# Attention in steps of two key blocks, the query projection held back by one chunk, and another tile order in the last chunk

## The chip, the core and the metric

The kernel runs on one core of one Trainium2 chip. The metric is the device time of one execution in microseconds (us). Engines are named as in the profile: PE multiplies matrices, PEld loads its weights, DVE, ACT and POOL work elementwise, SP issues the DMAs.

## What is computed

Two layers work on 1040 tokens (16 learned ones ahead of 1024) of 1024 features. Each layer has a normalisation, one input projection, two groups of attention heads, gates and an output projection. Cut to what matters here:

```python
hn = rmsnorm(h, norm_gain[l])
dq, dk, dv, dg, fq, fk, fv, ff, fg = split(hn @ w_in[l])
# differential heads (4): two softmaxes, one subtracted from the other
p = softmax(dq @ dk.T * scale, masked by chunks of 64)
a = p[:, :, 0] - lam * p[:, :, 1]
do = rmsnorm(a @ dv, subln_gain[l]) * (1 - lam_init) * silu(dg)
# forgetting heads (8): one softmax with a bias per key, causal by token
s = fq @ fk.T * scale + cum_logf(query) - cum_logf(key)
fo = softmax(s, causal) @ fv * silu(fg)
h = h + concat(do, fo) @ w_out[l]
```

Matrix products are made from split operands: a value is written as hi + lo, and hi*hi, lo*hi and hi*lo are added up.

## The kernel before

The tokens are cut into nine tiles (`BS`, the first of 80 tokens, the next seven of 128, the last of 64) and these into three chunks c of three tiles. The heads come in eight pairs p: 0 to 3 are the differential heads (the "diff" stage), 4 to 7 hold two forgetting heads each (the "fox" stage), which the code tells apart by s. A **unit** (l, p, c, s) is the attention of one chunk of queries against its 3, 6 or 9 blocks of keys.

For a unit, `scores` makes the products of queries and keys of one query tile into PSUM buffers named sc (three of them), in up to three pieces. DVE adds the bias and keeps a running minimum (L629), ACT takes the exponential and its sum (L633), DVE the reciprocal (L636). In the fox stage POOL scales the row (L665). In the diff stage there are two such rows for a tile; POOL scales the one (L679) and DVE joins them (L681). The result stands in e. Then, for each block j of keys, `transp` turns the three tiles' parts of e on PE into one of two PSUM buffers tp; ACT copies them out as ath (L710) and DVE makes the rest atl (L711). `av` multiplies these by the values into po.

In the diff stage the fill's k and q are rotated on DVE (L400 to L403) with a table that a DMA loads into cb. What stands around all this on PE is the **fill**: products of the projections (pj) that the next pairs and the gates need. `fills` makes them in the order of `ORDER`, k, q, gate and v of each pair, and then the output projection, in portions of two of eight k-steps (six products). `layer` walks through `attention`, which yields a time that its next step needs and a key; by a clock of its own (`pe.t`) `layer` puts in fill until that time has come, or while a credit lasts. A fill generator that may not go on yields True, and then nothing is put in. It may not go on, among others, where q of pair p and chunk c would overwrite the buffer `qls[c]`, of which there is one for each chunk; the line is

```python
while c and p and (p - 1, c - 1) not in box["sc_ok"]:
```

where `sc_ok` holds the chunks whose scores are all in. The order of PE is the one in which these calls are made; the other engines' order comes from the framework's scheduler, and each engine works through its own in order.

In `attention` one unit's blocks run as t0 t1 a0 t2 a1 t3 and so on (t a transposition, a the products with v), and after every second step one score step of the next unit is put in, as far as buffers of e are there (`free`). A unit starts when its last scores are through (`u.ready`).

Of the kernel before, what the change touches and what calls it, by code (L numbers as in the profile page):

```python
# [49 lines left out]

LS0, LS1, LT, L1S, LROT, LFOX = 2.04, 0.0045, 2.41, 4.87, 6.0, 5.61
OT1, OT2, OT3, OW, OL = 2.46, 4.57, 2.54, 7.53, 4.52
CMAX, SLACK, RMIN, RMAX, STEP, FR0, FR1 = 3.17, 0.8, 0.03, 2.52, 2, 2, 2
COST = {"k": 10.4, "q": 10.4, "g": 10.4, "v": 24.0, "h": 0.0}
FADD = [0.0, -2.7, 0.0, 2.0, 0.0, 0.2, -0.7, 47.4]
ATT = [21.5, 21.5, 21.2, 21.5, 28.5, 28.5, 28.1, 28.9]
# [24 lines left out]
def trunk_kernel(ctx, tc, x, meta, norm_gain, w_in, fbias, lq1, lk1, lq2, lk2,  # L81
# [356 lines left out]
    def q_unit(l, p, acts, box):  # L438


        diff = p < 4
        q0 = (DQ if diff else FQ) + (p % 4) * P
        ws = load_w_all(w_in[l], [(q0, q0 + P)])
        for c in range(3):
            w = CE[c] - CS[c]
            while c and p and (p - 1, c - 1) not in box["sc_ok"]:
                yield True
            mb, o = [], skip(l, c)
            yield from mtile(ws, acts, c, mb, o)
            src, scale = (rotate(mb[0], c, -SCALE, o), 1.0) if diff else (mb[0], -SCALE)  # L450
            qq = [st("qq", CW, F32R, QB) for _ in range(2)]
            ql = qls[c]
            if o:
                for t in qq + ql:
                    nc.gpsimd.memset(t[:, :o].bitcast(F32), 0.0)
            for s in range(2):
                r, ro = halves(s)
                split(qq[s][r, o:w], ql[s][r, o:w], src[r, o:w], scale)
                nc.gpsimd.tensor_scalar(qq[s][ro, o:w], qq[s][r, o:w].bitcast(F32), 1.0, 1.0,  # L459
                                        ALU.mult, ALU.mult)  # L460
            box["q", p, c] = (qq, ql)
            when["q", p, c] = pe.t + (LROT if diff else LFOX)
            yield
# [175 lines left out]
    class Unit:  # L639


        def __init__(self, l, p, s, c, box):
            self.l, self.p, self.s, self.c, self.box = l, p, s, c, box
            self.w = CE[c] - CS[c]
            self.at = []
            self.tiles = range(3 * c, 3 * c + 3)
            self.nblk = 3 * c + 3
            self.diff = p < 4
            self.ev = {}
            self.ready = 0.0  # L650
            self.begun = False
# [4 lines left out]
        def score(self, j, m):  # L656
# [5 lines left out]
            if not self.diff:  # L662
                cb = self.box["cb", self.s]
                e, r, rows = scores(kt, q, self.s, j, ext, lambda a, b: cb[:, a:b], True)
                nc.gpsimd.tensor_scalar(e[rows, :ext], e[rows, :ext], r[rows, 0:1], 1.0,  # L665
                                        ALU.mult, ALU.mult)
                self.at.append((e, rows))
                self.ready = pe.t + LS0 + LS1 * ext
                return
            dm = self.box["dm"]  # L670
# [4 lines left out]
            if m == 0:  # L675
# [4 lines left out]
                                    neglam[rows, l:l + 1], ALU.mult, ALU.mult)  # L680
            nc.vector.scalar_tensor_tensor(e0[rows, :ext], e0[rows, :ext], r0[rows, 0:1],  # L681
                                           e[rows, :ext], ALU.mult, ALU.add)
            self.at.append((e0, rows))
            self.ready = pe.t + LS0 + 1.3 * LS1 * ext

        def geom(self, j):
# [9 lines left out]
        def transp(self, j):  # L696
            c, w = self.c, self.w
            kz, i0, n0, n1 = self.geom(j)
            tp = att_ps()
            for i in reversed(range(i0, 3 * c + 3)):  # L700
                e, rows = self.at[i - 3 * c]
                o = BS[i] - CS[c] - self.pad(i)
                tr(tp[:kz, o:BE[i] - CS[c]], e[rows, BS[j] - self.pad(j):BE[j]],
                   ident[rows, rows])
# [67 lines left out]
    def attention(l, box):  # L772
# [5 lines left out]
        def score(u, step):  # L778
            if not u.begun:
                u.begun = True  # L780
                if u.c == 0 and u.s == 0:
                    box["sp"] = u.p
                    for s in range(0 if u.diff else 2):
                        cb = box["cb", s] = big("cb", 2)
                        h = 2 * (u.p - 4) + s
                        dma(out=cb, in_=cscr[l, h:h + 1, :].to_broadcast([P, T]))
            u.score(*step)
# [8 lines left out]
        for i, u in enumerate(units):  # L796
# [5 lines left out]
            if nx and nx.p != u.p and not nx.diff:  # L802
                free = 0
            n = u.nblk
            seq = [("t", j) for j in range(TB)]
            for j in range(n):
                seq.append(("a", j))
                if j + TB < n:
                    seq.append(("t", j + TB))
            nt = 0  # L810
            yield u.ready, ("v", u.p, 0)
            box["vp"] = u.p
            for k, (what, j) in enumerate(seq):
                if late and pe.t >= late[0][0]:
                    late.pop(0)[1]()
                    yield 0.0, None
                if what == "t":
                    u.transp(j)
                    nt += 1
                else:  # L820
                    yield u.ev[j][2], ("v", u.p, j)
                    u.av(j)
                yield 0.0, None
                if todo and (nt == n or (free > 0 and nt >= FR0 and k % FR1 == FR1 - 1)):
                    free -= 1
                    yield 0.0, ("k", nx.p, nx.c)
                    yield 0.0, ("q", nx.p, nx.c)
                    score(nx, todo.pop(0))
                    yield 0.0, None
            for t0, f in late:  # L830
                yield t0, None
                f()
# [319 lines left out]
```

## Time and profile before

| | |
|---|---|
| median of 3 runs | 1616.0 us (1613.42 to 1619.95) |
| the profiled execution | 1615.97 us, its span 1614.2 us |
| granted TensorE clock, mean | 0.961 |
| PE busy | 1490.0 us, 92% |
| DVE, ACT, POOL busy | 1044.3, 825.2, 772.6 us |

Layer 0 has its diff stage at about 94 to 415 us, its fox stage at 415 to 694 us, layer 1 its own at 876 to 1203 and 1203 to 1484 us; between and behind them lies the output projection. A row of a timeline has start, duration, engine, line, operation, output and inputs with their forms, the count of merged instructions, and in brackets the idle time of the engine before it with what ended it. A PE duration holds the latency of the array too; the distance of two starts tells what one costs in a stream.

### The profile page before, as it was taken

To read this page: it belongs to the slowest core of one execution; us is meant where nothing else is said; L and a number is where in the kernel's file an instruction comes from. 1 tells how busy PE (TensorE), PEld (TensorE's weight loads), DVE (VectorE), ACT (ScalarE), POOL (GpSimd) and SP (SyncE) were. 2 spreads that over 40 slices of the span, in tenths; PEclk is the share of its full clock that TensorE was granted. 3 is DMA by queue.
4 is the path that set the end of the run, shared out by engine and by line. 5 is a ranking of instruction groups with operands and counts; after the bars stand their busy time and mean duration, and the time that the engine had idled before them with its cause. 6 is when DMAs were issued, how large, how long until landed. Compare 5 with 4: busy or idle time off the path is not lost.

```text
span 1614.2 us, 30133 instructions
## 1 busy us (share of the span) xinstructions
PE 1490.0 (92%) x9932; PEld 1425.6 (88%) x9932; DVE 1044.3 (65%) x3020; ACT 825.2 (51%) x2067; POOL 772.6 (48%) x1211
## 2 busy tenths in 40 slices
PE   5979999999999999798997989999999999988997
PEld 4878998899999999697987989898999999977897
DVE  6468677856665556667755765876667555656654
ACT  6445445544555556544333544554446555555553
POOL 3355355523543445375746443544345344545564
PEclk8999999999999999799998999999999999998899
DMA  8322122213220222554524221322122112253454
GB/s 248 76 74 71 50 71 62 73 26 47 62 61 23 66 65 79 156 173 133 165 66 93 55 77 26 90 54 62 31 67 50 46 43 75 58 151 92 119 168 135
DMA packets 170317, 134.80 MB, mean 84 GB/s; under 512 B 18456, under 2 KB 165456, under 8 KB 170160
## 3 DMA queue, kind: packets, MB, share of 16 engines
q1 hardware_dynamic: 170160, 132.87, 31.2%
q8 instruction: 79, 1.29, 0.3%
q14 instruction: 78, 0.64, 0.1%
HBM read 111.49 MB, written 21.33 MB: 82 GB/s over the span
## 4 chain that ended last, share of the span: by engine, by line
PE 68%; DVE 11%; DMA 7%; issue 5%; POOL 4%; ACT 3%; SPq 1%; DVEq 0%; POOLq 0%; ACTq 0%
PE pj L161 43%; PE sc L161 9%; PE po L161 8%; PE tp L165 7%; DMA cb<-in_rope_dram 3%; DMA tc<-nscr 2%; DVE e L629 2%; DVE kt L410 2%; DVE e L681 2%; DVE tc L383 1%; ACT e L633 1%; DMA e<-in_x_dram 1%; POOL wlo L245 1%; DMA wst<-in_w_in_dram 1%; PE sc L165 1%
## 5 line engine op out<-in xcount | busy, mean ns | idle before, releaser
L161 PE MATMUL pj<-acth,whi 128*128 128x320 f32 (+2 forms) x1536 | 515.7, 336 | 3.6 <-DVE hc L895 2.1
L161 PE MATMUL pj<-actl,whi 128*128 128x320 f32 (+2 forms) x1536 | 497.4, 324 | 0.1
L161 PE MATMUL pj<-acth,wlo 128*128 128x320 f32 (+2 forms) x1536 | 496.8, 323 | 0.0
L633 ACT ACTIVATE e<-e,mn 80x80 f32<-80x80 f32 (+8 forms) x288 | 225.4, 783 | 165.2 <-DVE mn L629 158.0
L161 PEld LDWEIGHTS pj<-acth,whi 128*128 128x128 f32 x1536 | 294.7, 192 | 6.1 <-POOL whi L243 2.6
L161 PEld LDWEIGHTS pj<-acth,wlo 128*128 128x128 f32 x1536 | 294.3, 192 | 0.6
L161 PEld LDWEIGHTS pj<-actl,whi 128*128 128x128 f32 x1536 | 293.2, 191 | 0.7 <-DVE actl L410 0.6
L245 POOL TENSOR_TENSOR wlo<-wst,whi 128x256 fp32r<-128x256 f32 (+1 forms) x320 | 248.4, 787 | 81.5 <-ACT whi L241 69.2
L710 ACT ACTIVATE ath<-tp 128x320 fp32r<-128x320 f32 (+8 forms) x432 | 167.1, 402 | 171.9 <-PE tp L165 165.7
L711 DVE TENSOR_TENSOR atl<-tp,ath 128x320 fp32r<-128x320 f32 (+8 forms) x432 | 190.4, 449 | 98.6 <-ACT ath L710 94.9
L165 PE MATMUL tp<-ident,e 128*128 128x128 f32 (+2 forms) x1080 | 184.0, 280 | 50.0 <-DVE e L681 27.9
L161 PE MATMUL sc<-kt,qq 128*128 128x296 f32 (+9 forms) x480 | 178.8, 375 | 18.7 <-POOL qq L459 13.7
L165 PEld LDWEIGHTS tp<-ident,e 128*128 128x128 f32 (+2 forms) x1080 | 137.7, 141 | 59.0 <-issue 24.3
L665 POOL TENSOR_SCALAR e<-e,rl 80x80 f32<-80x80 f32 (+2 forms) x144 | 110.9, 770 | 157.1 <-DVE rl L636 154.4
L241 ACT ACTIVATE whi<-wst 128x256 fp32r<-128x256 f32 (+1 forms) x304 | 123.6, 413 | 104.1 <-PE pj L161 66.2
L629 DVE CUSTOM_DVE_ANT_0 e<-sc,cb 128x336 f32<-128x336 f32 (+8 forms) x272 | 139.8, 515 | 52.7 <-PE sc L161 49.9
L161 PE MATMUL po<-ath,v 128*128 128x256 f32 (+5 forms) x576 | 168.8, 334 | 4.0 <-ACT ath L710 2.1
L161 PE MATMUL pj<-whi,acth 128*128 128x256 f32 (+3 forms) x576 | 166.2, 289 | 4.3 <-DVE v L410 3.7
L161 PE MATMUL pj<-wlo,acth 128*128 128x256 f32 (+3 forms) x576 | 163.3, 284 | 1.3 <-POOL wlo L245 0.7
L161 PE MATMUL pj<-whi,actl 128*128 128x256 f32 (+3 forms) x576 | 163.2, 283 | 1.3 <-POOL actl L386 1.1
L161 PE MATMUL sc<-kt,ql 128*128 128x296 f32 (+9 forms) x480 | 161.9, 339 | 0.0
L161 PE MATMUL po<-atl,v 128*128 128x256 f32 (+5 forms) x432 | 137.7, 319 | 8.0 <-DVE atl L711 5.8
(153 smaller groups left out, 2513.6 us busy)
## 6 DMA issues: line engine op xcount, KB each, us to landing
wst<-in_w_in_dram SPq DMA_DIRECT2D x256, 128.0 KB
wst<-in_w_out_dram SPq DMA_DIRECT2D x192, 128.0 KB
cb<-cscr SPq DMA_DIRECT2D x16, 520.0 KB
cb<-in_rope_dram SPq DMA_DIRECT2D x20, 320.0 KB
cb<-in_rope_dram SPq DMA_DIRECT2D x16, 384.0 KB
cb<-in_rope_dram SPq DMA_DIRECT2D x12, 336.0 KB
e<-in_x_dram SPq DMA_DIRECT2D x7, 512.0 KB
actl<-oscr SPq DMA_DIRECT2D x4, 768.0 KB
```

The lines of the kernel that those rows point to most:

```text
L161: nc.tensor.matmul(o, a, b, start=start, stop=stop)
L165: nc.tensor.transpose(o, a, idn)
L241: nc.scalar.activation(hi, sg_, AF.Copy)
L245: eng.tensor_tensor(lo, sg_, hi.bitcast(F32), ALU.subtract)
L383: nc.vector.scalar_tensor_tensor(t[:, :w], src, ng[:, l, k:k + 1], rb, ALU.mult, ALU.mult)
L410: nc.vector.tensor_tensor(lo, src, hi.bitcast(F32), ALU.subtract)
L629: nc.vector.tensor_tensor_reduce(e[rows, a:b], pt[rows, :b - a], bias(a, b)[rows, :], op0=ALU.add, op1=ALU.min, scale=1.0, scalar=3e38 if ...
L633: nc.scalar.activation(e[rows, :ext], e[rows, :ext], AF.Exp, scale=-1.0, bias=mn[rows, len(pcs) - 1:len(pcs)], accum_out=l[rows, 0:1])
L665: nc.gpsimd.tensor_scalar(e[rows, :ext], e[rows, :ext], r[rows, 0:1], 1.0, ALU.mult, ALU.mult)
L681: nc.vector.scalar_tensor_tensor(e0[rows, :ext], e0[rows, :ext], r0[rows, 0:1], e[rows, :ext], ALU.mult, ALU.add)
L710: nc.scalar.activation(ah[:kz, n0:w], tp[:kz, n0:w], AF.Copy)
L711: nc.vector.tensor_tensor(al[:kz, n0:w], tp[:kz, n0:w], ah[:kz, n0:w].bitcast(F32), ALU.subtract)
```

## The change

Three things. In `attention` a step is now two blocks wide: the products of two blocks one behind the other, then at once the transpositions of the next two, then one score step of the next unit (two in the diff stage). A late sum of a finished unit (`late`) comes behind the transpositions, no longer ahead of them. In `q_unit` the projection of q for chunk c waits until the scores of the pair before are in for this chunk, no longer for the one ahead of it. In the last chunk the query tiles are scored in the order 6, 8, 7, and every unit transposes its tiles in the order of their scores, where it was the reverse.

```diff
@@ q_unit
-            while c and p and (p - 1, c - 1) not in box["sc_ok"]:
+            while p and (p - 1, c) not in box["sc_ok"]:
                 yield True
@@ Unit.__init__
-            self.tiles = range(3 * c, 3 * c + 3)
+            self.tiles = (6, 8, 7) if c == 2 else range(3 * c, 3 * c + 3)
@@ Unit.transp
-            for i in reversed(range(i0, 3 * c + 3)):
-                e, rows = self.at[i - 3 * c]
+            for i in self.tiles:
+                if i < i0:
+                    continue
+                e, rows = self.at[i]
@@ attention
-            for k, (what, j) in enumerate(seq):
-                if late and pe.t >= late[0][0]:
-                    late.pop(0)[1]()
-                    yield 0.0, None
-                if what == "t":
-                    u.transp(j)
-                    nt += 1
-                else:
-                    yield u.ev[j][2], ("v", u.p, j)
-                    u.av(j)
-                yield 0.0, None
-                if todo and (nt == n or (free > 0 and nt >= FR0 and k % FR1 == FR1 - 1)):
+            for j0 in range(0, n + 1, TB):
+                done, group = range(max(j0 - TB, 0), j0), range(j0, min(j0 + TB, n))
+                for j in done:
+                    if j < n:
+                        yield u.ev[min(done[-1], n - 1)][2], ("v", u.p, j)
+                        u.av(j)
+                for j in group:
+                    u.transp(j)
+                yield 0.0, None
+                if late and pe.t >= late[0][0]:
+                    late.pop(0)[1]()
+                    yield 0.0, None
+                for _ in range(2 if nx and nx.diff else 1):
+                    if todo and (free > 0 or j0 + TB >= n):
...
+                        score(nx, todo.pop(0))
...
+            if n % TB:
+                yield u.ev[n - 1][2], ("v", u.p, n - 1)
+                u.av(n - 1)
```

Three places show what this makes of the engines' order. The first is PE in layer 0 ahead of unit (0, 6, 2, 0), the last chunk of pair 6; tp are the transpositions, pj is fill, po the products with v, sc the scores. Before, these rows stand at the start of the unit, and between its last score and here lie 30 products of fill:

```order
L161 MATMUL pj<-acth_249,whi 128x336
L161 MATMUL pj<-acth_249,wlo 128x336
L161 MATMUL pj<-actl_250,whi 128x336
L165 MATMUL tp<-ident,e 80x128 x3
L165 MATMUL tp<-ident,e 128x128 x3
L161 MATMUL sc<-kt,qq 128x424
L161 MATMUL sc<-kt,ql_85 128x424
```

After:

```order
L161 MATMUL sc<-kt,qq 128x488
L161 MATMUL sc<-kt,ql_84 128x488
L161 MATMUL sc<-kt,qq 128x488
L161 MATMUL sc<-kt,ql_84 128x488
L161 LDWEIGHTS cb_68
L161 MATMUL sc<-cb_68 128x128
L161 MATMUL po<-ath,v 128x256
L161 MATMUL po<-atl,v 128x256
L161 MATMUL po<-ath,v 128x256
L161 MATMUL po<-atl,v 128x256
L165 MATMUL tp<-ident,e 80x128 x3
L165 MATMUL tp<-ident,e 128x128 x3
```

The unit's last scores (tile 7) now stand four products of 256 columns ahead of its first transposition, and the fill is gone from there. The second place is PE in layer 0 at the start of pair 5, unit (0, 5, 0, 0). Before, the last scores of its tile 2 are followed by fill, 18 products of it up to the first transposition:

```order
L161 MATMUL sc<-kt,qq 128x336
L161 MATMUL sc<-kt,ql_80 128x336
L161 LDWEIGHTS cb_68
L161 MATMUL sc<-cb_68 128x128
L161 MATMUL pj<-acth_362,whi 128x384
L161 MATMUL pj<-acth_362,wlo 128x384
L161 MATMUL pj<-actl_363,whi 128x384
```

After:

```order
L161 MATMUL sc<-kt,qq 128x336
L161 MATMUL sc<-kt,ql_80 128x336
L161 LDWEIGHTS cb_68
L161 MATMUL sc<-cb_68 128x128
L165 MATMUL tp<-ident,e 80x80
L165 MATMUL tp<-ident,e 80x128 x2
L165 MATMUL tp<-ident,e 128x128 x2
```

Nothing stands between scores and transpositions any more. The third place is DVE in layer 0 behind the first two transpositions of unit (0, 1, 1, 0), a diff unit, where the scores of tile 6 follow on PE; atl is the rest of a transposed block, ms a sum per head, L629 takes a piece of the scores out of PSUM. Before:

```order
L711 TENSOR_TENSOR atl<-tp,ath 80x384
L629 ISA e,mn<-sc,cb 128x424
L629 ISA mn 128x1
L711 TENSOR_TENSOR atl<-tp,ath 128x384
L629 ISA e,mn<-sc,cb,mn 128x424
```

After (L711 is L714 there, L770 is L773):

```order
L714 TENSOR_TENSOR atl<-tp,ath 80x384
L773 COPY ms<-sc 80x1
L773 COPY ms<-sc 128x1
L714 TENSOR_TENSOR atl<-tp,ath 128x384
L773 COPY ms<-sc 128x1
L629 ISA e,mn<-sc,cb 128x424
L629 ISA mn 128x1
```

The first piece of the scores now stands behind both blocks' atl and the three copies.

## Rows read from the trace of the kernel before

**Rows 1.** The page: span, then busy time, share and count of PE.

```profile
span 1614.2 us, 30133 instructions
PE 1490.0 (92%) x9932; PEld 1425.6 (88%) x9932; DVE 1044.3 (65%) x3020; ACT 825.2 (51%) x2067; POOL 772.6 (48%) x1211
```

**Rows 2.** By stage: stretch, length, busy time (count) of PE, PEld, DVE, ACT, POOL; clock.

```profile
94.00:415.00 321.00, 302.84 (x2039) 294.16 (x2040) 231.66 (x684) 164.19 (x421) 146.02 (x205) 0.97 0.25 59
415.00:655.00 240.00, 237.79 (x1651) 227.04 (x1650) 141.31 (x449) 132.56 (x337) 109.70 (x196) 1.00 0.22 60
655.00:694.00 39.00, 27.68 (x158) 24.30 (x157) 26.74 (x79) 20.96 (x53) 17.44 (x33) 0.78 0.53 161
...
1203.00:1444.00 241.00, 237.69 (x1661) 227.05 (x1660) 142.43 (x451) 133.94 (x339) 111.90 (x208) 1.00 0.25 65
```

**Rows 3.** Who PE waited for: us in total, times, longest.

```profile
PE tp L165 <- DVE e L681: 27.9, 11, 3.9
PE tp L165 <- POOL e L665: 21.9, 5, 6.3
...
PE po L161 <- DVE atl L711: 5.8, 8, 2.9
```

**Rows 4.** Timeline of PE around unit (0, 6, 2, 0).

```profile
612.48 0.44 PE L161 MATMUL po<-atl,v 80*128 80x384 f32 x1 [0.33 <-DVE atl L711]
...
613.99 0.23 PE L161 MATMUL sc<-cb 128*128 128x128 bf16 x1
...
622.17 0.82 PE L165 MATMUL tp<-ident,e 128*80 128x128 f32 x6
```

**Rows 5.** Timeline of POOL there, the scaling of tile 7.

```profile
617.65 1.09 POOL L665 TENSOR_SCALAR e<-e,rl 128x976 f32<-128x976 f32 x1
```

**Rows 6.** Timeline ahead of unit (0, 5, 0, 0).

```profile
487.03 0.28 PE L161 MATMUL po<-ath,v 128*128 128x256 f32 x1
...
487.14 0.28 PE L161 MATMUL po<-atl,v 128*128 128x256 f32 x1
...
487.58 0.23 PE L161 MATMUL sc<-cb 128*128 128x128 bf16 x1
...
489.99 0.54 POOL L665 TENSOR_SCALAR e<-e,rl 128x336 f32<-128x336 f32 x1
```

**Rows 7.** Timeline of PE: the longest start of a unit of pair 7, layer 0.

```profile
677.70 1.08 PE L165 MATMUL tp<-ident,e 128*80 128x128 f32 x4 [5.58 <-POOL e L665]
```

**Rows 8.** Busy time in stretches of low granted clock, columns as in Rows 2.

```profile
309.40:316.20 6.80, 4.89 (x20) 4.86 (x21) 6.40 (x16) 2.63 (x6) 3.49 (x5) 0.50 0.25 63
244.50:247.90 3.40, 3.40 (x15) 3.38 (x15) 3.25 (x10) 2.08 (x6) 2.67 (x4) 0.50 0.25 89
```

**Rows 9.** Timeline: starts of diff units, and DVE ahead of the one at 311 us.

```profile
243.76 0.50 PE L165 MATMUL tp<-ident,e 128*80 128x128 f32 x3 [2.31 <-DVE e L681]
...
308.23 0.51 DVE L402 TENSOR_TENSOR tc<-tc,cb 128x336 f32<-128x336 f32 x1 [0.95 <-DMA cb<-in_rope_dram]
...
309.86 1.30 DVE L681 SCALAR_TENSOR_TENSOR e<-e,rl 128x1040 f32<-128x1040 f32 x1
...
311.31 1.47 PE L165 MATMUL tp<-ident,e 128*80 128x128 f32 x6 [3.88 <-DVE e L681]
```

**Rows 10.** Timeline of PE and DVE at the first blocks of unit (0, 0, 1, 0).

```profile
122.73 0.83 PE L165 MATMUL tp<-ident,e 128*80 128x128 f32 x6
122.91 0.28 DVE L770 COPY ms<-sc 80x1 f32<-80x1 f32 x3 [0.43 <-PE sc L161]
...
123.32 0.44 PE L161 MATMUL sc<-kt,qq 128*128 128x424 f32 x1
...
123.79 0.55 DVE L711 TENSOR_TENSOR atl<-tp,ath 80x384 fp32r<-80x384 f32 x1 [0.60 <-ACT ath L710]
123.79 0.36 PE L161 MATMUL sc<-kt,qq 128*128 128x424 f32 x1
...
124.26 0.58 DVE L629 CUSTOM_DVE_ANT_0 e<-sc,cb 128x424 f32<-128x424 f32 x1
```

More of the change, by code (lines that the diff above doesn't have):

```diff
@@ L52 @@
 OT1, OT2, OT3, OW, OL = 2.46, 4.57, 2.54, 7.53, 4.52
-CMAX, SLACK, RMIN, RMAX, STEP, FR0, FR1 = 3.17, 0.8, 0.03, 2.52, 2, 2, 2
+CMAX, SLACK, RMIN, RMAX, STEP = 3.17, 0.8, 0.03, 2.52, 2
 COST = {"k": 10.4, "q": 10.4, "g": 10.4, "v": 24.0, "h": 0.0}
@@ L644, in __init__ @@
             self.w = CE[c] - CS[c]
-            self.at = []
-            self.tiles = range(3 * c, 3 * c + 3)
+            self.at = {}
+            self.tiles = (6, 8, 7) if c == 2 else range(3 * c, 3 * c + 3)
             self.nblk = 3 * c + 3
@@ L666, in score @@
                                         ALU.mult, ALU.mult)
-                self.at.append((e, rows))
+                self.at[j] = e, rows
                 self.ready = pe.t + LS0 + LS1 * ext
@@ L682, in score @@
                                            e[rows, :ext], ALU.mult, ALU.add)
-            self.at.append((e0, rows))
+            self.at[j] = e0, rows
             self.ready = pe.t + LS0 + 1.3 * LS1 * ext
@@ L804, in attention @@
             n = u.nblk
[L805 to L810, printed above, removed]
             yield u.ready, ("v", u.p, 0)
             box["vp"] = u.p
-            for k, (what, j) in enumerate(seq):
+            for j0 in range(0, n + 1, TB):
[7 more added lines that the diff above has]
+                yield 0.0, None
                 if late and pe.t >= late[0][0]:
@@ L816, in attention @@
                     yield 0.0, None
-                if what == "t":
-                    u.transp(j)
-                    nt += 1
-                else:
-                    yield u.ev[j][2], ("v", u.p, j)
-                    u.av(j)
-                yield 0.0, None
-                if todo and (nt == n or (free > 0 and nt >= FR0 and k % FR1 == FR1 - 1)):
[L825 to L828, printed above, removed]
-                    yield 0.0, None
+                for _ in range(2 if nx and nx.diff else 1):
+                    if todo and (free > 0 or j0 + TB >= n):
+                        free -= 1
+                        yield 0.0, ("k", nx.p, nx.c)
+                        yield 0.0, ("q", nx.p, nx.c)
+                        score(nx, todo.pop(0))
[3 more added lines that the diff above has]
+                u.av(n - 1)
+                yield 0.0, None
             for t0, f in late:
```

## The prediction

> **What bounds the kernel now.** I read the page first, then busy time by stage, then who PE waited for, then the timeline at the starts of units. PE is busy for 92% of the span [rows 1], and the stages show where the other 8% lies. In both fox stages up to pair 7 PE is busy for 237.8 of 240 us and for 237.7 of 241, at clock 1.00 [rows 2]: nothing is left to be won there, and whatever is added to PE's waits comes out in full. In the diff stage it is 302.8 of 321 us, so 18 are idle, and in pair 7 of layer 0 27.7 of 39 at clock 0.78 [rows 2]. The waits have one main form: at the start of a unit the first transposition waits for its e, 27.9 us in 11 waits for DVE's L681 (diff) and 21.9 in 5 for POOL's L665 (fox) [rows 3]. Each of the long ones draws a stretch at half the clock behind it [rows 8]. So the question is whether the change shortens the starts of the diff units and pair 7, and what it does to the full fox stages.
>
> **The change part by part**, against the profiled execution's 1615.97 us, which is 0.03 off the median, so no correction is needed.
>
> *Products and transpositions in pairs.* The same instructions are issued. Six transpositions in a row take 0.59 us until the next product starts, 0.1 each [rows 10], and this run of six stands at the start of every unit of before already; pairing saves nothing and costs nothing in itself. (The Trainium skill, "TensorE: Matmul & The Clock Gate", Part 4, says that the full clock doesn't engage for transpositions; the fox stages at 1.00 speak against that here. Were it to decide, it is the fourth rival below.)
>
> *What the pair has to wait for.* Before, between block j's transposition and its product stood the product of the block ahead and the transposition of the block behind; now both blocks of a pair have only scores and fill between. In the planner each pair therefore asks for fill, and so fill is used earlier inside a unit and is short at the starts. Where no fill comes, the atl chain shows: the nearest row is 0.33 us [rows 4]. The order has 32 fox pairs with no fill between. Between nothing (the scores of the next unit cover it) and 0.5 us, I take 0.25: 8 us, from 0 to 16.
>
> *The starts of fox units.* This is the main term. By the order, the PE work between a unit's last score and its first transposition falls in six starts from 3 to 6 us to nearly nothing. Three are last chunks, (0,6,2,0), (1,4,2,0) and (1,6,2,0): q of pair 7 or 5 has come to its last chunk, which the new line lets on only when all scores of the pair are in, so no fill is there. Before, that start came without a wait: the score of tile 7 began its last product at 613.99, e was ready at 617.65 + 1.09 = 618.74 [rows 5], 4.75 us later, and PE had work until 622.17 [rows 4]. Now there is 0.04 for that product, four products of 256 columns at 0.11 each [rows 6], and two transpositions ahead of the one that waits, 0.22: 0.7 us of cover, so a wait of 4.0. Three times: 12 us. At (0,4,2,0) twelve products of fill stay, some 2.1 us of cover: 1.9. At the start of pairs 5 (both layers) and 7 (layer 0) the order has nothing between tile 2's scores and the transpositions: 487.58 to 489.99 + 0.54 = 490.53 is 2.95 us [rows 6], less 0.04 and 0.2 of transpositions: 2.7, three times 8.1. Together 22 us, from 17 (all chains a fifth shorter) to 26.
>
> *The clock behind them.* After a wait of 3.9 us PE ran 6.8 us at 0.50, busy for 4.89 of them, so about 2.4 were lost; after one of 2.3 us it ran 3.4 us at 0.50 and lost 1.7 [rows 8, 9]. Three starts at 2.4 and three at 1.7, the latter not always: 11 us, from 5 to 18.
>
> *Scores in pairs in the diff stage.* In unit c = 1 four pieces of scores now follow each other, and there are three sc buffers. In before the first piece's L629 started 0.94 us after the scores did, with one atl ahead of it [rows 10]; now a second atl (0.55) and three copies (0.28) stand ahead [rows 10]. So its end is at about 0.94 + 0.55 + 0.28 + 0.58 = 2.35 us. The fourth piece asks at 3 times 0.47 = 1.4, and some 0.3 later since the three late sums now stand ahead of the scores: a wait of 0.6 us, eight units, 5 us. Bounds: 0, if other work of PE comes between, and 10.
>
> *Starts of the diff units.* Starts of a first chunk lose or gain cover by the order, from 2.1 us less to 0.9 more, six of them: together 3 us more, from 0 to 6. Starts of a last chunk: the tile that comes last is now 976 keys wide in two pieces, no longer 1040 in three, and its scores stand two steps earlier, while DVE's order still has the rotation's L402, which waits for its table, ahead of the joining of e, as at 308.23 and 309.86 [rows 9]. By the order the starts of pair 1 have four fewer DVE instructions in between, the others as many as before. I take 4 us off, bounds 14 off and 5 on.
>
> *Pair 7.* Its long waits, 5.6 us as the longest of layer 0 [rows 7], stay, since the fill is still used up. The output projection's loads and splits move two to four blocks ahead, so the first start gets the crowd on DVE and the next two lose some: 3 us off, bounds 8 off and 3 on.
>
> *Tile order.* In other units tiles are transposed in the order of their scores, so up to two transpositions, 0.2 us, cover the last tile; that is counted above. An e buffer is free no earlier.
>
> Sum: 8 + 22 + 11 + 5 + 3 - 4 - 3 = 42 us, so 1616 + 42 = **1658 us**.
>
> **The rivals.** *First: the diff starts decide, and it gets faster.* The order of DVE at pair 1 speaks for it, and that last scores come earlier; against it, that e there waits on the rotation's table, which the change doesn't touch. If all 27.9 us of L681 waits [rows 3] went, and with them five low stretches (half of some 26 us, 13), while the fox starts cost their lower 17 and 7 of clock: 1616 - 41 + 24 = 1599 us. It decides if at least two thirds of the diff waits go. *Second: no change.* Fill that is not used at the starts is used later, and pair 7's idle time, 11 of 39 us in layer 0 [rows 2] and about as much in layer 1, shrinks by as much as the new waits add: 1616 to 1622, say 1618. For it: the total of fill is the same, and the work behind the last unit of layer 0 is the same by the order. Against it: pair 7 starts with the fill used up in both orders. *Third: worse.* Each new wait, the short ones too, draws a full 6.8 us at half the clock, and DVE's queue, which had 141 us of work in 240 in the fox stage [rows 2], runs behind in pairs without fill: 22 becomes 30, 11 becomes 25, 8 becomes 20, some 1616 + 85 = 1700. *Fourth: transpositions let the clock fall.* If longer runs of them did what long waits do, each of the 192 pairs (8 in each of the 24 sets of three chunks) would cost 1.7 us of half clock [rows 8]: 326 us, 1942. The run of six at clock 1.00 [rows 2, 10] is against it. (That is the rule of the Trainium skill, "TensorE: Matmul & The Clock Gate", Part 4.)
>
> **How the numbers follow.** Forecast 0.74, first rival 0.09, second 0.10, third 0.06, fourth 0.01. About 0.5% is what a measurement of this kernel can tell from no change: 8 us, so 1608 and 1624 are the limits. The forecast's own lower end is 8 us or so above 1616, with the fox starts at 17, 5 of clock and the gains in the diff stage large (1630 to 1688, most of it). Below 1608 lies the first rival: 0.09. Between them the second, less a little: 0.09. Above: 0.82. The range leaves out the first, third and fourth rival and part of the second: 1622 to 1690.
>
> **What would show it.** In the profile of the changed kernel: PE busy for some 95% of the fox stages, at a clock below 1.00; PE's waits for L665 at 40 us or more, in 10 or 11 waits, the new ones at last chunks of pairs 4 and 6 near 4 us; waits of sc for DVE's L629 about 5 us more; waits of tp for DVE's joining (L682 there) between 15 and 30. The forecast is wrong if L665's waits stay near 22 us (then the cover at the starts is not what the order seems to say), or if the waits for L682 fall below 10.

## The result, and the profile after

The changed kernel takes **1657.6 us** (median of 4 runs, 1655.15 to 1659.49) against 1616.2 before: a ratio of 1.025 (95% interval 1.023 to 1.027). The forecast was 1658, with slower at 0.82. The total came out to the microsecond; of the terms that make it up some hold and some don't, and the misses offset each other.

The page of the kernel after, to be held against [rows 1]: the span, then busy time, share and count of PE.

```profile
span 1657.7 us, 30114 instructions
PE 1515.8 (91%) x9932; PEld 1435.1 (87%) x9932; DVE 1037.1 (63%) x3020; ACT 823.6 (50%) x2067; POOL 767.5 (46%) x1211
```

The same number of instructions on PE, 43.5 us more span. The stages, columns as in [rows 2]; the last two rows begin later than there, since pair 7 of layer 0 now starts at 673 us and the fox stage of layer 1 at 1230:

```profile
94.00:415.00 321.00, 303.98 (x2028) 294.26 (x2026) 227.76 (x679) 162.44 (x414) 139.46 (x200) 0.97 0.24 58
415.00:655.00 240.00, 228.21 (x1545) 214.34 (x1544) 132.05 (x425) 125.21 (x319) 104.09 (x181) 0.99 0.19 53
673.00:712.00 39.00, 26.27 (x118) 21.28 (x117) 25.09 (x75) 18.99 (x49) 14.22 (x24) 0.65 0.44 131
1231.00:1472.00 241.00, 227.73 (x1540) 212.57 (x1539) 133.98 (x425) 124.44 (x318) 102.57 (x187) 0.99 0.20 52
```

The diff stage reads as before. In the fox stage of layer 0 PE, busy for 237.8 of 240 us before, is now busy for 228.2, and what counts more, it gets through 1545 products in that time instead of 1651, 6.4% less: 15 us of work. In layer 1 it is 1540 in 241 us instead of 1661. Pair 7 of layer 0 gets through 118 in its first 39 us instead of 158, at a clock of 0.65 instead of 0.78. Who PE waited for, as in [rows 3]:

```profile
PE tp L165 <- POOL e L666: 34.0, 22, 3.5
PE sc L161 <- POOL qq L459: 21.1, 7, 5.9
PE tp L165 <- DVE e L682: 16.5, 10, 2.9
PE po L161 <- DVE atl L714: 13.0, 26, 1.1
...
PE sc L161 <- DVE mn L629: 4.3, 7, 1.1
...
PE po L161 <- ACT ath L713: 3.6, 8, 0.7
...
PE sc L161 <- DVE ms L773: 2.5, 7, 0.7
```

Transpositions of fox units wait for POOL's scaling in 22 waits instead of 5, products for atl in 26 instead of 8; the diff starts (L682, L681 before) fall from 27.9 to 16.5.

The idle time in such a list is not the whole cost of a wait, so the sizes below are taken **from start to start**: the time by which a PE instruction starts later after its predecessor than such a neighbour usually does, where that is over 0.15 us, added up by kind of instruction. The timeline around unit (0, 6, 2, 0) shows the difference:

```profile
639.06 0.39 PE L161 MATMUL po<-ath,v 128*128 128x256 f32 x1 [0.32 <-ACT ath L713]
...
640.21 0.39 PE L161 MATMUL po<-atl,v 128*128 128x256 f32 x1 [0.76 <-DVE atl L714]
640.44 0.28 PE L161 MATMUL po<-ath,v 128*128 128x256 f32 x1
640.55 0.31 PE L161 MATMUL po<-atl,v 128*128 128x256 f32 x1
640.70 0.38 PE L165 MATMUL tp<-ident,e 128*80 128x128 f32 x2
...
642.49 0.64 PE L165 MATMUL tp<-ident,e 128*80 128x128 f32 x4 [1.41 <-POOL e L666]
```

Two such products start 0.11 apart in a stream (640.44, 640.55), here 1.15: the wait cost 1.04, of which 0.76 stands in brackets. The bracket begins where the record of the product before ends, after 0.39 us, while in a stream the next one would have started after 0.11: the difference, 0.28, stands in no bracket. (The Trainium skill, "Trainium Kernel Development and Optimization", section Performance Expectations, calls the busy time of matrix products a bad measure because they are pipelined, and names that of the weight loads as a good one. The fox stage agrees: PE's busy time fell by 9.6 us in 240, PEld's by 12.7, the work done by 15.)

The same rows are the predicted bare start of a last chunk: the last four transpositions stand right behind two others and wait. But this start cost 1.6 us, not 4.0: part of the chain to e had passed in the atl waits just ahead of it.

The start of pair 5, unit (0, 5, 0, 0), all engines:

```profile
499.28 0.23 PE L161 MATMUL sc<-cb 128*128 128x128 bf16 x1
...
499.35 0.23 PE L165 MATMUL tp<-ident,e 80*80 80x80 f32 x1
...
499.82 0.42 DVE L245 TENSOR_TENSOR wlo<-wst,whi 128x256 fp32r<-128x256 f32 x1
...
500.69 0.48 DVE L752 TENSOR_TENSOR ta<-po,ta 64x320 f32<-64x320 f32 x1
...
501.31 0.86 POOL L755 TENSOR_TENSOR ta<-ta,gs 64x320 f32<-64x320 f32 x1 [2.34 <-issue]
...
502.28 0.96 POOL L666 TENSOR_SCALAR e<-e,rl 128x208 f32<-128x208 f32 x2
...
502.77 0.31 PE L165 MATMUL tp<-ident,e 128*80 128x128 f32 x1 [3.19 <-POOL e L666]
```

Nothing of PE's stands between the last score (499.28) and the transpositions, as the order said, and the finish of the unit before (L752, L755) stands inside the chain to e: 3.8 us from start to start, where 2.7 were forecast. At pair 7 of layer 0 it is the output projection:

```profile
675.94 0.51 DVE L883 TENSOR_TENSOR tc<-actl,tc 128x336 f32<-128x336 f32 x1 [0.77 <-DMA tc<-nscr]
...
677.20 0.31 PE L165 MATMUL tp<-ident,e 128*80 128x128 f32 x1 [3.34 <-POOL e L666]
678.27 0.51 DVE L883 TENSOR_TENSOR tc<-actl,tc 128x336 f32<-128x336 f32 x1 [1.75 <-DMA tc<-nscr]
...
679.73 0.65 PE L165 MATMUL tp<-ident,e 128*80 128x128 f32 x2 [2.22 <-POOL e L666]
```

Two multiplications that wait for a DMA (L883) stand ahead of the reciprocals of tiles 1 and 2 in DVE's queue, and the start costs 6.3 us.

The low clock, columns as in [rows 8]; the first two follow the starts of pair 7 in the two layers, the third that of pair 5:

```profile
677.60:704.90 27.30, 18.15 (x63) 13.92 (x64) 17.00 (x51) 12.21 (x31) 8.68 (x15) 0.50 0.47 145
1490.00:1517.30 27.30, 19.11 (x67) 14.48 (x68) 16.13 (x50) 12.32 (x33) 8.17 (x15) 0.50 0.34 109
503.50:506.90 3.40, 3.40 (x18) 3.37 (x17) 1.07 (x5) 1.26 (x4) 0.58 (x2) 0.50 0.06 14
```

All stretches at half clock add up to 142 us (129 before), and PE is busy in them for 107 us instead of 89: half of the difference, some 9 us, is lost. The fox starts that waited 1.3 to 1.6 us left no low stretch.

What nobody had priced stands in the diff stage. A first score of the next pair, PE, first in the kernel before, then in the changed one:

```profile
153.38 0.82 PE L165 MATMUL tp<-ident,e 128*80 128x128 f32 x6 [2.11 <-DVE e L681]
...
156.17 0.34 PE L161 MATMUL sc<-kt,qq 128*80 128x256 f32 x1 [0.92 <-POOL qq L459]
```

```profile
152.42 0.31 PE L161 MATMUL pj<-actl,whi 128*128 128x320 f32 x1
156.17 0.50 PE L161 MATMUL sc<-kt,qq 128*80 128x256 f32 x1 [3.44 <-POOL qq L459]
```

Before, the unit ahead waits for its e at 153.38, and the score waits 0.92 us. After, the unit ahead has no such wait, PE meets the same wall behind it, q that isn't ready, and the score starts at the same 156.17.

### The profile page after: what moved, and what is told of

Its sections match the earlier page's. It is cut to its first block, busy times and chain, and to the rows that moved or that the text cites. A ratio compares the mean times of both kernels' runs of the same rounds, so it can differ in the third digit from the quotient of the medians.

```text
span 1657.7 us, 30114 instructions
## 1 busy us (share of the span) xinstructions
PE 1515.8 (91%) x9932; PEld 1435.1 (87%) x9932; DVE 1037.1 (63%) x3020; ACT 823.6 (50%) x2067; POOL 767.5 (46%) x1211
## 4 chain that ended last, share of the span: by engine, by line
PE 66%; DVE 11%; DMA 7%; issue 6%; POOL 5%; ACT 3%; SPq 0%; POOLq 0%; DVEq 0%; ACTq 0%
PE pj L161 42%; PE sc L161 9%; PE po L161 8%; PE tp L165 6%; DVE e L629 2%; DMA cb<-in_rope_dram 2%; DMA tc<-nscr 2%; DVE atl L714 2%; POOL tc L401 1%; POOL wlo L245 1%; ACT e L633 1%; DVE e L682 1%; DMA wst<-in_w_in_dram 1%; DVE kt L410 1%; DMA wst<-in_w_out_dram 1%
## 5 line engine op out<-in xcount | busy, mean ns | idle before, releaser
L714 DVE TENSOR_TENSOR atl<-tp,ath 128x320 fp32r<-128x320 f32 (+8 forms) x432 | 184.9, 448 | 104.2 <-ACT ath L713 102.1
L713 ACT ACTIVATE ath<-tp 128x320 fp32r<-128x320 f32 (+8 forms) x432 | 157.4, 402 | 154.3 <-PE tp L165 149.6
L165 PE MATMUL tp<-ident,e 128*128 128x128 f32 (+2 forms) x1080 | 168.9, 280 | 50.6 <-POOL e L666 34.0
L161 PE MATMUL sc<-kt,qq 128*128 128x296 f32 (+9 forms) x480 | 179.9, 377 | 27.7 <-POOL qq L459 21.1
L666 POOL TENSOR_SCALAR e<-e,rl 80x80 f32<-80x80 f32 (+2 forms) x144 | 111.6, 776 | 169.6 <-DVE rl L636 162.6
L165 PEld LDWEIGHTS tp<-ident,e 128*128 128x128 f32 (+2 forms) x1080 | 131.1, 139 | 62.6 <-POOL e L666 39.4
L629 DVE CUSTOM_DVE_ANT_0 e<-sc,cb 128x336 f32<-128x336 f32 (+8 forms) x272 | 139.5, 515 | 59.9 <-PE sc L161 57.1
L161 PE MATMUL po<-ath,v 128*128 128x256 f32 (+5 forms) x576 | 160.0, 322 | 5.8 <-ACT ath L713 3.6
L161 PE MATMUL po<-atl,v 128*128 128x256 f32 (+5 forms) x432 | 140.1, 329 | 13.7 <-DVE atl L714 13.0
```

Source lines behind the costliest of these rows:

```text
L161: nc.tensor.matmul(o, a, b, start=start, stop=stop)
L165: nc.tensor.transpose(o, a, idn)
L629: nc.vector.tensor_tensor_reduce(e[rows, a:b], pt[rows, :b - a], bias(a, b)[rows, :], op0=ALU.add, op1=ALU.min, scale=1.0, scalar=3e38 if ...
L713: nc.scalar.activation(ah[:kz, n0:w], tp[:kz, n0:w], AF.Copy)
L714: nc.vector.tensor_tensor(al[:kz, n0:w], tp[:kz, n0:w], ah[:kz, n0:w].bitcast(F32), ALU.subtract)
```

## The experiments

All are compared with the kernel before on the same chip. The columns of the table are worked out from each profiled execution: time and ratio, the length of fox pairs 4 to 6 in the two layers (from the first transposition of (l, 4, 0, 0) to that of (l, 7, 0, 0)), and from start to start what products wait for ath and atl in the fox stages, what starts of fox units wait for e, what starts of diff units wait, what scores in the diff stage wait; the last is all time at half clock.

| kernel | us | ratio (95%) | pairs 4-6 | fox atl | fox starts | diff starts | diff scores | half clock |
|---|---|---|---|---|---|---|---|---|
| before | 1616.2 | | 240.2, 240.7 | 18.4 | 23.0 | 30.9 | 23.5 | 129 |
| after | 1657.6 | 1.025 (1.023-1.027) | 256.5, 255.2 | 34.4 | 38.9 | 18.4 | 37.1 | 142 |
| h1_diff | 1615.6 | 1.000 (0.998-1.002) | 241.1, 234.8 | 14.8 | 23.8 | 17.9 | 36.6 | 119 |
| h2_fox | 1657.9 | 1.026 (1.023-1.029) | 257.3, 257.3 | 32.7 | 38.0 | 17.0 | 28.4 | 152 |
| e3_tiles | 1611.7 | 0.998 (0.996-0.999) | 239.5, 237.6 | 15.4 | 21.1 | 18.6 | 29.4 | 125 |
| e5_steps | 1673.5 | 1.036 (1.033-1.039) | 268.6, 264.6 | 44.4 | 24.3 | 15.8 | 45.8 | 142 |
| e1_oldq | 1662.8 | 1.029 (1.025-1.033) | 265.5, 264.9 | 45.1 | 22.5 | 21.8 | 37.6 | 146 |
| g1_lt | 1638.8 | 1.014 (1.012-1.017) | 248.4, 246.1 | 42.5 | 13.4 | 16.4 | 38.4 | 118 |
| g5_lt08 | 1677.6 | 1.038 (1.037-1.040) | 261.9, 261.9 | 75.3 | 13.4 | 19.8 | 32.7 | 107 |
| g2_before_lt | 1620.5 | 1.003 (1.002-1.005) | 239.7, 238.1 | 23.2 | 15.5 | 27.0 | 24.7 | 112 |
| g3_tiles_lt | 1614.1 | 0.999 (0.998-1.001) | 240.2, 237.9 | 25.2 | 13.2 | 13.5 | 30.0 | 112 |
| m0_bufs | 1671.7 | 1.035 (1.032-1.039) | 259.1, 257.0 | 42.6 | 36.8 | 20.4 | 36.8 | 163 |
| m3_ahead | 1685.7 | 1.040 (1.035-1.046) | 260.5, 259.7 | 2.9 | 23.7, and 62.6 (below) | 19.9 | 36.7 | 156 |
| m4_stag | 1653.9 | 1.023 (1.020-1.027) | 245.2, 245.6 | 14.3 | 34.0 | 18.9 | 37.8 | 179 |

**Which stage pays: h1_diff and h2_fox.** The theory: the whole loss lies in the fox pairs. The rival: both stages pay. In h1_diff the loop of the kernel before stands beside the new one:

```diff
+            if u.diff:
                 for j0 in range(0, n + 1, TB):
...
+            else:
+                for k, (what, j) in enumerate(seq):
...
```

with the old q line; in h2_fox the condition is turned round, with the new q line.

> Pairs in the diff pairs only; fox pairs in single steps as before; new tile order, old q line. Main theory (all of the loss lies in the fox stages: 16 us of atl waits, 12 of starts, 3 of pair 7, 10 of clock; in the diff stage 13 us gained at starts stand against 14 lost at first scores): 1616 us, from 1610 to 1624, with atl waits of the fox stages back at about 18 us and the starts of pairs 4 to 6 at about 1. Rival (the diff stage itself pays for the pairs, at the scores that wait for q): 1626 to 1640. Second rival (a better start of the diff stage hands its gain on): under 1608.

> Pairs in the fox pairs only, the diff pairs in single steps; new tile order and new q line as in the changed kernel. If the loss lies in the fox pairs alone: 1653 to 1660 us, the changed kernel's time, or 4 us less, as the kernel before with the new tile order alone is 4 us faster than before (then also fewer waits of first scores for q, 29 instead of 37 us). If pairs of both stages act together (what the diff stage uses up is missing in fox): 1635 to 1648 us.

With pairs in the diff stage alone the time is that of the kernel before, with pairs in fox alone that of the changed kernel. h1_diff, PE's waits:

```profile
PE tp L165 <- POOL e L666: 21.6, 9, 5.9
...
PE po L161 <- DVE atl L714: 2.8, 5, 1.0
```

So the loss is that of the fox pairs, all of it. (h1_diff has the old line on q as well; e1_oldq below shows that it gains nothing by that.) In the diff stage what is changed cancels out: with tile order and pairs the starts give back 13 us and the scores take 13. Held against e3_tiles below, which lacks only the pairs, h1_diff is some 4 us slower: that is what pairs in the diff stage cost.

**The tile order: e3_tiles and e5_steps.**

```diff
+            self.tiles = (6, 8, 7) if c == 2 else range(3 * c, 3 * c + 3)
...
-            for i in reversed(range(i0, 3 * c + 3)):
+            for i in self.tiles:
```

e3_tiles adds this to the kernel before; e5_steps takes it (and the q line) out of the changed one.

> The kernel before with the new tile order alone (last chunk scored and transposed 1, 3, 2; other chunks transposed in the order of their scores); single steps and old q line. Theory A (the tile order brought the gain of the changed kernel at the last chunks of the diff pairs, 20.4 to 7.2 us of waits): these waits fall to about 8 here too, 13 us, and a few us of low clock with them: 1600 us, from 1594 to 1607. Theory B (it came from the scores of two pieces in one step, which stand earlier): waits of these starts stay at 18 to 21 us and the time at 1612 to 1620. Fox starts (0.7 us of waits in pairs 4 to 6) stay as they are in both.

> The pairs alone: the changed kernel with the old tile order and the old q line. By theory A (tile order brings the gain at the diff starts) it loses that gain, 13 us and some clock, against the kernel with the old q line: 1655 to 1665. By theory B (pairs bring it) it stands within 5 us of that kernel, 1637 to 1650. In both the atl waits of the fox stages (34 us in the changed kernel, 18 before) stay at 28 to 36 us, since a pair waits for both its atl.

The tile order alone shortens the starts of last chunks of diff units, from 20.4 to 10.6 us (7.2 in the changed kernel). So do the pairs alone, to 2.4 in e5_steps. Neither theory is right: either change does it, and either pays for it at the scores behind. Starts and scores of the diff stage together take 54.4 us before, 48.0 with the tile order, 55.5 in the changed kernel, 61.6 with the pairs alone. e3_tiles, PE's waits:

```profile
PE sc L161 <- POOL qq L459: 20.5, 7, 6.0
...
PE tp L165 <- DVE e L681: 16.6, 12, 2.9
```

The wait of scores for q, 13.7 us before, is at 20.5 with the tile order alone. So the tile order is worth 4 us, not 16, and no run here shows another part of the change to make the kernel faster (the line on q was not run with single steps). Both expectations of e5_steps were too low: the pairs alone lose 58 us, and their atl waits, expected at 28 to 36 us, are 44.4. Why that is 11 more than e1_oldq, which has the tile order, isn't shown beyond the 8 us more at the scores.

**The line on q: e1_oldq.**

```diff
-            while p and (p - 1, c) not in box["sc_ok"]:
+            while c and p and (p - 1, c - 1) not in box["sc_ok"]:
```

> The changed kernel with one line undone: q of the next pair may again be projected for a chunk as soon as the scores of the chunk ahead of it are in. Main theory (fill is missing at starts because the new line holds q back): the order then has 5 to 6 us of PE work again between the last score and the first transposition of (0,4,2,0), (0,6,2,0), (1,4,2,0) and (1,6,2,0), where the changed kernel waited 1.3 to 1.6 us each and about 1 us more for atl just ahead. 6 us of starts, some 3 of atl and up to four low stretches (1.7 each, 7) go: 1642 us, from 1637 to 1650. The starts of pairs 5 and 7 stay as bare as they are. Rival (fill is one sum: what is spent at these starts is missing later): 1655 to 1660, with longer waits in pair 7 or at (1,6,2,1).

The rival holds in the main: 1662.8 us, just above its 1655 to 1660, and from the changed kernel no difference that the intervals tell apart. The four starts of last chunks of pairs 4 and 6 have no wait any more and fox starts as a whole fall from 38.9 to 22.5 us; but atl waits grow from 34.4 to 45.1 and pairs 4 to 6 take 9 and 10 us longer, pair 7 some 8 and 6 less, where the rival had looked for longer waits in pair 7. PE's waits:

```profile
PE tp L165 <- POOL e L666: 17.9, 12, 2.5
PE po L161 <- DVE atl L714: 11.7, 21, 3.2
...
PE po L161 <- ACT ath L713: 7.2, 13, 2.4
```

The new line decides where the fill is missing, not how much.

**How much fill a pair asks for: g1_lt, g5_lt08, and g2_before_lt, g3_tiles_lt as controls.** The planner lets a product come 2.41 us after its block's transposition and puts fill between until then. One number is changed, to 1.6 (g1_lt) and 0.8 (g5_lt08) in the changed kernel, to 1.6 in the kernel before (g2_before_lt) and in e3_tiles (g3_tiles_lt):

```diff
-LS0, LS1, LT, L1S, LROT, LFOX = 2.04, 0.0045, 2.41, 4.87, 6.0, 5.61
+LS0, LS1, LT, L1S, LROT, LFOX = 2.04, 0.0045, 1.6, 4.87, 6.0, 5.61
```

> The changed kernel with one number of the planner smaller: the time it allows from a block's transposition to its product, 2.41 us, set to 1.6, so that it puts less fill into each pair. By the order PE work comes back to the starts that the change left bare: 5.9 us at (0,4,2,0) and (1,4,2,0), 5.6 at (0,6,2,0), 3.0 to 3.7 at the starts of pairs 5 and of pair 7. Theory of starts (the loss lies in where the planner puts the fill): the starts' waits go, 13 us in pairs 4 to 6 and some 10 in pair 7, with 5 to 10 of clock, and the atl waits grow by less than 8: 1630 to 1642 us. Theory of one sum (the real chain from transposition to product takes its time whatever the planner believes, and the fill is the same in sum; the old q line showed it: starts 16 us shorter, atl waits 11 longer, no gain): atl waits grow by as much as the starts lose: 1652 to 1664 us.

> The changed kernel with the number at 0.8. By the order 80 fox pairs have no fill between transposition and product (27 with 1.6, 32 with 2.41), and the starts have 3.1 to 7 us of PE work. Starts have hardly a wait left to lose (13 us with 1.6, of these 6 at the one start in each layer that stays bare). If a pair without fill costs what the nearest row of the kernel before says, 0.25 to 0.5 us, 53 more pairs bring 13 to 26 us of atl waits, less what the fill saves where it goes: 1642 to 1660. If the chain is covered anyway by scores: 1632 to 1640.

> The kernel before with that number alone (2.41 to 1.6), old tile order: the control for what the smaller number gives without pairs. In the changed kernel it gave 19 us. If that came because pairs ask for fill twice as hard, single steps gain less, through pair 7 alone: 1608 us, from 1602 to 1614. If the number was badly set for either order, some 15 to 20 us come here as well: 1597 to 1602.

> The kernel before with the new tile order (that kernel was 4 us faster than before) and with the planner's time from transposition to product at 1.6 instead of 2.41. By the order the starts of pair 7 gain PE work, 2.1 us at (0,7,0,1), 2.3 at (1,7,0,0) and 3.5 at (1,7,0,1), and elsewhere little changes. If those starts were short of fill only because the planner had put it between transpositions and products, their waits (21 us in pair 7) fall by 6 to 9 and the clock gives 3 to 5 more, against 3 to 5 us more of atl waits: 1604 us, from 1599 to 1609. If fill is one sum: 1609 to 1615.

g1_lt gives 19 us back, as the theory of starts said: the bare starts are covered again (pairs 4 to 6 wait 0.1 us, 13.0 in the changed kernel), half clock falls from 142 to 118 us, and the atl waits grow by 8. With 0.8 they grow by another 33, more than the 13 to 26 expected, and all is lost again (1677.6 us, expected 1642 to 1660). By the order 53 more fox pairs have no fill there; if all 33 us are theirs, such a pair costs 0.62 us, an estimate. Counted pair by pair, the products of pairs without fill wait longer than that, from start to start some 25 us in 32 pairs of the changed kernel (0.8 each), 34 in 27 of g1_lt (1.2) and 63 in 80 of g5_lt08 (0.8). PE's waits in g1_lt:

```profile
PE po L161 <- DVE atl L714: 22.3, 38, 2.5
...
PE tp L165 <- POOL e L666: 12.3, 4, 6.4
```

and in g5_lt08:

```profile
PE po L161 <- DVE atl L714: 28.7, 72, 1.8
...
PE tp L165 <- POOL e L666: 12.4, 5, 5.9
PE po L161 <- ACT ath L713: 10.8, 26, 1.6
```

In single steps the number gives nothing (g2_before_lt is 5 us slower than before, though 1608 was expected, g3_tiles_lt no faster than before though 1604 was): fox starts win 8 us there and atl and the projections take them. So the 19 us come with the pairs, which asked for more fill than was good for the whole: in g1_lt fox starts wait 25.5 us less and atl waits cost 8.1 more. The theory of one sum, which e1_oldq seemed to bear out, is too strong: in g1_lt the fill was worth more ahead of a start than inside a pair, and in g5_lt08, where too many pairs were left without, it wasn't.

**What a pair lacks: m0_bufs, m3_ahead, m4_stag.** In single steps a product and a transposition of other blocks stand between a block's transposition and its product; in pairs, only fill and scores. If that is the cause, products that lag behind the transpositions by a block should mend it, though both still come two by two. That takes a third buffer for ath and atl, which six qq buffers instead of eight make room for; m0_bufs, the control, has these buffers alone.

```diff
-WB, XB, QB, EB, AB, GB, OB, TCB = 8, 5, 8, 6, 2, 4, 3, 3
+WB, XB, QB, EB, AB, GB, OB, TCB = 8, 5, 6, 6, 3, 4, 3, 3
```

m3_ahead adds in fox

```diff
-                done, group = range(max(j0 - TB, 0), j0), range(j0, min(j0 + TB, n))
+                done = range(max(j0 - TB, 0), j0)
+                group = range(j0 + ah if j0 else 0, min(j0 + TB + ah, n))
...
-                        yield u.ev[min(done[-1], n - 1)][2], ("v", u.p, j)
+                        yield u.ev[j if ah else min(done[-1], n - 1)][2], ("v", u.p, j)
```

with ah = 1, and m4_stag, in place of it,

```diff
+            d0 = TB if u.diff else 1
...
+                done = range(max(j0 - 2 * TB + d0, 0), min(j0 - TB + d0, n)) if j0 else range(0)
                 for j in done:
+                    yield u.ev[min(done[-1], n - 1) if u.diff else j][2], ("v", u.p, j)
...
+            for j in sorted(u.ev):
+                yield u.ev[j][2], ("v", u.p, j)
+                u.av(j)
```

> Control for the next kernel: the changed kernel with three buffers each for ath and atl (two before) and six instead of eight for qq to make room. TensorE's order is that of the changed kernel. In pairs a third buffer has nothing to do: 1655 to 1662 us. If the copies wait for the buffers of ath and atl, the atl waits of the fox stages (34 us) fall by 10 or more.

> As the control, but in fox pairs the transpositions run one block further ahead: three blocks at the start, then products of blocks 0 and 1, transpositions of 3 and 4, products of 2 and 3, and so on; each product is due by its own block. Products and transpositions still stand in pairs, but between a block's transposition and its product there is always a product or two of other blocks. Theory (a pair loses what stood between a block's transposition and its product, one product and one transposition of another block, 0.3 to 0.5 us in each of some 100 pairs): atl waits in fox fall to 20 us or less and the starts get their fill back, 1615 to 1632 us. Rival (pairs as such, or the length of a run of transpositions, cost the time): within 8 us of the control.

> As m0_bufs (the control: three buffers for ath and atl, six for qq; 1671.7 us), but in fox pairs the products lag by one block: transpositions of blocks 0 and 1, product 0, transpositions 2 and 3, products 1 and 2, transpositions 4 and 5, and so on, each product due by its own block. Only two blocks stand transposed ahead at the start, so the wait of the third transposition for a tp buffer, which cost m3_ahead what it had won, should go. Theory (a pair loses what stood between a block's transposition and its product): atl waits of the fox stages, 42.6 us from start to start in the control and 2.9 in m3_ahead, come to 25 or less, and the fill that pairs no longer ask for helps the starts: 1640 to 1655 us. Rival (two blocks in a row cost it whatever stands between, or the two tp buffers pass the wait on to the transpositions): within 6 us of the control, with what the products no longer wait found at the transpositions.

The control missed its expectation: 14 us slower than the changed kernel, with 8 us more of atl waits. Most of it lies outside the fox pairs: its profiled execution, the slowest of its four, is 21 us longer than that of the changed kernel, 8 of them ahead of the first transposition of layer 0, 8 in the diff stage of layer 0, and 2.6 and 1.8 in pairs 4 to 6. Whether that is the fewer qq buffers or the other order of the elementwise engines stays open. It stands as the base for the other two.

m3_ahead is no faster than its control, as the rival said (1.040, from 1.035 to 1.046, against 1.035, from 1.032 to 1.039), but not for the rival's reason. Its waits of PE, then its PE at the start of unit (0, 5, 2, 0):

```profile
PE tp L165 <- DVE atl L714: 53.2, 51, 2.7
```

```profile
565.09 0.82 PE L165 MATMUL tp<-ident,e 128*80 128x128 f32 x6
568.39 0.55 PE L165 MATMUL tp<-ident,e 128*128 128x128 f32 x3 [2.48 <-DVE atl L714]
```

Products wait 2.9 us for atl instead of 42.6. In their place the third block's transposition, which stands ahead of every product of the unit, waits for one of the two tp buffers in each of the 48 fox units, 62.6 us from start to start. m4_stag takes that start away and keeps the lag:

```profile
PE po L161 <- DVE atl L714: 4.3, 5, 1.7
...
PE tp L165 <- DVE atl L714: 1.6, 5, 0.6
```

Pairs 4 to 6 fall from 259 and 257 us to 245 and 246, the atl waits from 42.6 to 14.3, though 92 fox pairs have no fill (32 in the control), and the time by 1.2% against the kernel before, 1.035 to 1.023, some 19 us, as the theory expected. The gain lies where the theory put it: of the 26.6 us between the two profiled executions 25.3 are in pairs 4 to 6. So most of what the pairs cost there is the missing block in between, not the run of two, which m4_stag keeps; 5 us in each layer are left. It isn't quite one step alone: m4_stag also makes each product due by its own block. And it is no faster than the changed kernel (1.023 against 1.025): outside pairs 4 to 6 it takes 15 us more than that, as its control, with the same buffers, takes 16 more. Its half clock, 179 us, is the highest of all; why stays open.

## Why the prediction was right, and where its steps weren't

The forecast's mechanism is what happened: pairs use the fill up inside the units, and starts of fox units stand bare. That the total came out to the microsecond is luck: the measured terms add up to 42 us as the forecast ones do, with the waits for atl and the scores of the diff stage 8 and 9 us above their forecast and the other five together 17 below theirs. By its terms, from start to start:

| term of the sum | forecast (bounds) | measured |
|---|---|---|
| pairs that wait for atl | 8 (0 to 16) | 16.0 |
| bare starts of fox units | 22 (17 to 26) | 18.7 |
| clock behind them | 11 (5 to 18) | 9 |
| scores in pairs, diff stage | 5 (0 to 10) | 13.6 |
| first-chunk starts, diff (six) | 3 (0 to 6) | 1.4 |
| last-chunk starts, diff | -4 (-14 to 5) | -13.2 |
| pair 7, other starts | -3 (-8 to 3) | -3.6 |

- **Pairs and atl.** The step took 32 pairs without fill at 0.25 us, from a row with 0.33 us in brackets [rows 4]. The count held (32 in the trace as well), the price was less than half of what came. A bracket isn't what a wait costs (0.76 in brackets was 1.04 above), and a pair without fill came to 0.62 by the estimate from g5_lt08 and to 0.8 pair by pair. The upper bound, 16, is what came.
- **Starts of fox units.** The sum held, its parts didn't. The three last chunks were put at 4.0 us each and cost 1.6, since the chain from [rows 5] was shorter (4.0 us from score to transposition instead of 4.75) and the atl waits ahead had used part of it; (0, 4, 2, 0) was put at 1.9 and cost 1.3. The first chunks of pairs 5 and 7 were put at 2.7 each and cost 3.8, 2.6 and 6.3: the chain of [rows 6] was taken as if nothing else stood in its queues, and now the finish of the unit ahead and the output projection's waits for DMA stood in it. Where cover goes, the neighbours in the other engines' queues come closer too.
- **The line on q** was named as the cause of the bare last chunks. It is (e1_oldq covers them) and it costs nothing: without it the fill is missing in the pairs instead. That step priced a place as if the fill were lost and not moved.
- **Clock.** 2.4 us behind each long wait was right for none of the last chunks (they waited too little), 1.7 for the starts of pair 5, and pair 7 made up for it with 27.3 us of low clock in each layer (17.1 and 20.5 before). Nor does each long start draw such a stretch: in the kernel before, those of 2.8, 2.3 and 2.3 us at 106, 153 and 965 us drew none.
- **Scores in the diff stage.** The mechanism that was forecast is there but small, and shows at the copies of the late sums (L773) and not at L629, whose waits are 4.3 us (4.8 before): scores wait for these copies seven times, each time in a c = 1 unit as forecast, 2.5 us in brackets and 3.0 from start to start, where 5 were put down. What the step left out is the larger part of the 13.6 us, scores that come earlier and wait for q (13.7 us in brackets before, 21.1 after); 6 of the 13.6 come with the tile order alone. The lower bound for the last-chunk starts was nearly reached, and the two cancel. A start that gets shorter in front of a producer that doesn't is moved, not won.
- **The rivals.** The first (diff starts decide) had its condition met in part: 11.4 of 27.9 us of the waits for e went, and it needed two thirds; in h1_diff, where 11.9 went and the fox stage kept its single steps, the scores took it back. The second (fill that is not used at the starts is used later) is what e1_oldq shows for fill moved between pairs and starts, and it fails for the change as a whole; m4_stag, whose products wait less with less fill ahead of them, is in line with a pair needing more fill than two single steps. The third (each short wait draws a stretch at half clock; its own figures add up to 1692, not 1700) fails: the fox starts of 1.3 to 1.6 us drew none. The fourth (transpositions let the clock fall) fails: with 128 of the 192 pairs in them the fox stages run at 0.99. (That rule of the Trainium skill, "TensorE: Matmul & The Clock Gate", Part 4, does not show here.)
- **The signs to look for.** PE busy for 95% of the fox stage: 95.1 and 94.5, at 0.99. L665's waits (L666 in the changed kernel) of 40 us or more in 10 or 11 waits: 34.0 in 22, short of it, since many are short. L682's between 15 and 30: 16.5. L629's 5 us more: no, 0.5 less, and 2.5 at L773.

## What to carry to other kernels

When steps are made wider, look at what stood between a producer and its consumer in the narrow order: here one product and one transposition of other blocks, and where no fill took their place, a pair without them waited some 0.6 to 1.2 us. Fill that hides latencies is one budget: price a change by whether it asks for more of it, not by the place where it first runs out, and then check where the planner's numbers send it, since here a smaller request of the pairs, which sent fill to the starts, was worth 19 us. And a wait that gets shorter counts only if the next producer in line is ready: sum the waits of a stage over its kinds before a gain is booked.

## What was not expected of the hardware

- A wait of PE costs more than its bracket, 1.04 against 0.76 us above; between stages the count of products in equal time shows the loss (6.4% fewer) where PE's busy time shows 4%.
- In pairs 4 to 6 many short waits went with the full clock. g5_lt08 has 72 waits for atl and ath there, none above 0.9 us, and a granted clock of 1.00; the changed kernel has 29 of these and nine for e, the longest 3.2 us, and 0.99. Over the whole execution g5_lt08 has the least half clock of all, 107 us against 142. g5_lt08 in the two fox stages, columns as in [rows 2]:

```profile
416.00:678.00 262.00, 247.12 (x1618) 223.68 (x1617) 140.82 (x448) 129.53 (x335) 109.00 (x196) 1.00 0.20 55
1230.00:1490.00 260.00, 245.19 (x1612) 221.81 (x1611) 138.90 (x442) 129.76 (x335) 109.88 (x205) 1.00 0.20 52
```
